# Mean square from token-major x, the phases' low part on ScalarE, the scan's last quarter behind three quarters of the GLU, and more warm matmuls

## Chip, cores and metric

One core of a Trainium2 chip runs the whole program. The metric is the device time of one launch in microseconds, the median of several runs.

## What is computed

A decoder block on 256 tokens of width 1024, in float32: an RMS norm, one wide input projection, causal attention of 8 heads beside a diagonal state-space scan (S5) with a gated linear unit, both merged by sigmoid gates, an output projection and a squared-ReLU MLP of width 4096, and a last RMS norm. Of the reference, cut:

```python
def rms_norm(x, g):
    y = xf * lax.rsqrt(jnp.mean(xf * xf, axis=-1, keepdims=True) + RMS_EPS)
    return (y * g.astype(jnp.float32)).astype(x.dtype)
...
h = rms_norm(x, g_mix)
z = h @ w_in            # q, k, v, u (scan input), two gates
a = moba_attention(rotary(q), rotary(k), v)     # one block of 256: plain causal
s = s5_branch(u, ...)   # scan, then gelu(y) @ w_glu, one half gates the other
x = x + (sigmoid(g_a) * a + sigmoid(g_b) * s) @ w_out
x = x + squared_relu(rms_norm(x, g_mlp) @ w_up) @ w_down
return rms_norm(x, g_final)
```

## The kernel before, in words

Each float32 product is made of three products in the type fp32r: a weight `w` is cast to `hi` on ScalarE (ACT, L83), VectorE (DVE) subtracts it to get `lo` (L84), the activations are split the same way, and TensorE (PE) adds hi·hi, hi·lo and lo·hi (`mm3` L87, `tok_mm` L264). A weight comes in units of 128x1024 float32 (512 KB) on SyncE's (SP's) DMA queue, in order (`w_load` L68), into five buffers; `hi` and `lo` have four buffers each.

The norm's scale is not applied to x. `xgh` and `xgl` are x times the gain, channel-major (`xT`), and the projections of them are multiplied by the tokens' factor `rs` behind the product. So PE can start before the mean square is known. The mean square is made from channel-major x: five ACT squares and three DVE additions into `sq` (L184 to L188), then PE multiplies the two remaining slices by a column of ones (`ms`, L202 to L206). DVE scales it into `rsm` (L208) and makes a first guess of the inverse root, GpSimd (POOL) does three Newton steps (`rsqrt`, L191); from it come `rs_half` (DVE, L213) and `rs_ps`, a broadcast by PE (L216).

The order of the program is: warm matmuls on zeros (L152), the scan's input projection `u` in eight slices of k (L160 to L182), then the steps of the string `ORDER` (L45): V is the projection `v` in units v00 to v03 (chunk 0) and v4 to v7 (chunk 1); P prepares the scan's coefficients (`prepare`, L358, some hundred 128x16 DVE operations named `s`, and the transposes `bt`, L470); T makes tables of cosines and sines (`tables`, L511); C is the second part of the coefficients; Q is a quarter of the scan (`ssm_quad`, L529); K are queries and keys with their rotation, S the scores, A the attention's output, G and B the gates; X loads a table of ACT functions, Y is the gelu of the scan's output. Then follow the GLU's quarters (L644), `w_out`, `w_up`, `w_down`.

A scheduler orders the instructions of each engine from this program order, from priorities (`tc.high_priority`, which the splits of weights have, with SPLIT_PRIO, and the Newton steps, with RSP) and from its own costs; each engine then runs its list in order. So an instruction that waits holds all that stand behind it on its engine.

The tables' phases are time times turn, in two parts. ACT writes the high part (L515), DVE takes the nearest whole turn from it (L516, L517), and adds the low part with four operations of 128x128 a table (L519).

Of the kernel before, what the change touches and what calls it, by code (L numbers as in the profile page):

```python
# [8 lines left out]
F32 = mybir.dt.float32  # L9
# [28 lines left out]
HEAT = 7  # L38
# [7 lines left out]
         "B0 G3 S3 X1 Y0 A3 B1")  # L46


def build(ctx, tc, dr, out):
# [93 lines left out]
    ones = keep.tile([P, 1], F32, name="ones")  # L143
    V.memset(ones, 1.0)
# [89 lines left out]
    V.tensor_mul(rcos, cos_c, rs)  # L234
    V.tensor_mul(rsin, sin_c, rs)
# [65 lines left out]
    scale = P ** -0.5  # L301
    mixA = p1.tile([P, KD, T], F32, name="mixA")

    def attn_head(q, k, j):
# [8 lines left out]
        V.tensor_reduce(st[:, 0:1], s[:, 0:128], axis=mybir.AxisListType.X, op=ALU.max)  # L313
        V.tensor_reduce(st[:, 1:2], s[:, 128:384], axis=mybir.AxisListType.X, op=ALU.max)
        V.tensor_scalar(st[:, 0:2], st[:, 0:2], -scale, None, op0=ALU.mult)
        pr = p1.tile([P, 384], F32, tag="pr", bufs=2, name="pr")
        act(pr[:, 0:128], s[:, 0:128], AF.Exp, bias=st[:, 0:1], scale=scale,
                     accum_out=st[:, 2:3])
        act(pr[:, 128:384], s[:, 128:384], AF.Exp, bias=st[:, 1:2], scale=scale,
# [281 lines left out]
    for step in ORDER.split():  # L601
# [24 lines left out]
        elif part == "Y":  # L626
            gelu()
# [16 lines left out]
    for q in range(4):  # L644
        acc = wide_banks(f"glu{q}") if q % 2 else [flat(mm_bank(f"glu{q}{h}")) for h in range(2)]
        for kk_ in range(2):
            wh, wl = w_unit(dr["w_glu"][2 * q + kk_], f"glu{q}{kk_}")
            for k2 in range(2):
                k, w = 2 * kk_ + k2, slice(k2 * 512, (k2 + 1) * 512)
                for hf in range(2):  # L650
                    tok_mm(acc[hf], wh[:, w], wl[:, w], yhl[0][:, 0:4], yhl[0][:, 4:8], k, hf,
                           k == 0, k == 3)
# [12 lines left out]
        split(mxh[:, two, :], mxl[:, two, :], mixA[:, two, :])  # L665
    ph1.__exit__(None, None, None)
# [213 lines left out]
```

## Time and profile before

| | |
|---|---|
| median of 3 runs | 404.85 us (404.71 to 405.25) |
| the profiled execution | 405.1 us, its span 403.2 us |
| PE busy | 394.3 us, 98% of the span |
| weight loads of PE | 355.2 us, beside the matmuls |
| DVE busy | 292.8 us, 73% |
| ACT busy | 225.9 us, 56% |
| POOL busy | 30.3 us, 8% |
| read from memory | 69.18 MB, 174 GB/s over the span |

The busy shares are averages over stages that differ. A row of the timeline gives the start of a group of like instructions, the time from the first one's start to the last one's end, their number, and in brackets how long the engine was idle before it and what released it. Matmuls overlap, so the distance from one start to the next is shorter than a row's duration; the same holds, by less, for DVE's and ACT's instructions.

### The profile page before, as it was taken

What the parts mean: (1) busy time and instruction counts of PE and PEld (TensorE: products, weight loads), DVE (VectorE), ACT (ScalarE), POOL (GpSimd) and SP (SyncE); (2) the same over time, 40 slices, a digit from 0 to 9 for tenths busy, and PEclk for the clock granted to TensorE, in tenths of its full rate; (3) what the DMA queues carried; (4) which work ended last, traced back from release to release, by engine and by line L of the source; (5) the groups of instructions that cost most, each with busy time, mean ns of one, the idle gap of its engine ahead of it and who ended that gap; (6) DMA issues with size and microseconds to landing.
All of it is one profiled execution on the core that took longest, in us unless ns stands there. A gap on an engine that the chain in (4) does not pass through costs nothing.

```text
span 403.2 us, 6862 instructions
## 1 busy us (share of the span) xinstructions
PE 394.3 (98%) x2635; PEld 355.2 (88%) x2635; DVE 292.8 (73%) x520; ACT 225.9 (56%) x360; POOL 30.3 (8%) x39
## 2 busy tenths in 40 slices
PE   8999999999999999999999999999999999999993
PEld 5988898989899787888889999999999888889983
DVE  5999999999999994769748665656565443564425
ACT  6767977655276557945647645464546334353323
POOL 4151492000000000000000000000000000000000
PEclk9999999999999999999999999999999999999998
DMA  8994843354516252456486465554555565555202
GB/s 228 401 337 149 246 154 102 111 202 151 192 56 208 84 195 102 158 159 206 161 308 209 152 215 191 176 194 172 191 178 193 172 205 169 199 192 178 101 0 104
DMA packets 23199, 71.57 MB, mean 178 GB/s; under 512 B 2944, under 2 KB 5248, under 8 KB 23168
## 3 DMA queue, kind: packets, MB, share of 16 engines
q1 hardware_dynamic: 20144, 68.92, 50.6%
q10 hardware_dynamic: 3024, 2.23, 1.9%
q8 instruction: 20, 0.33, 0.3%
q14 instruction: 11, 0.09, 0.1%
HBM read 69.18 MB, written 1.05 MB: 174 GB/s over the span
## 4 chain that ended last, share of the span: by engine, by line
PE 84%; DVE 5%; DMA 4%; ACT 2%; POOL 2%; issue 1%; ACTq 1%; SPq 0%; DVEq 0%
PE up L89 8%; PE up L90 8%; PE up L88 8%; PE dn L735 6%; PE dn L734 6%; PE dn L733 6%; PE k L88 2%; PE k L89 2%; PE k L90 2%; PE gb L268 2%; PE gb L266 2%; PE gb L267 2%; PE glu L268 2%; PE glu L266 2%; PE dnq L733 2%; PE dnq L735 2%
## 5 line engine op out<-in xcount | busy, mean ns | idle before, releaser
L89 PE MATMUL up<-x2l,hi_up 128*128 128x256 f32 x256 | 72.5, 284 | 0.0
L90 PE MATMUL up<-x2h,lo_up 128*128 128x256 f32 x256 | 72.3, 283 | 0.0
L88 PE MATMUL up<-x2h,hi_up 128*128 128x256 f32 x256 | 71.8, 283 | 0.0
L84 DVE TENSOR_TENSOR lo_dn<-raw_dn,hi_dn 128x1024 fp32r<-128x1024 f32 x32 | 39.2, 1225 | 44.0 <-ACT hi_dn L83 44.0
L83 ACT CAST hi_dn<-raw_dn 128x1024 fp32r<-128x1024 f32 x32 | 33.5, 1048 | 51.6 <-PE dn L735 25.8
L84 DVE TENSOR_TENSOR lo_up<-raw_up,hi_up 128x1024 fp32r<-128x1024 f32 x32 | 38.8, 1223 | 27.7 <-ACT hi_up L83 27.7
L83 ACT CAST hi_up<-raw_up 128x1024 fp32r<-128x1024 f32 x32 | 33.3, 1046 | 39.2 <-PE up L89 18.5
L89 PEld LDWEIGHTS up<-x2l,hi_up 128*128 128x128 f32 x256 | 49.1, 192 | 0.2 <-DVE x2l L694 0.2
L90 PEld LDWEIGHTS up<-x2h,lo_up 128*128 128x128 f32 x256 | 49.1, 192 | 0.0
L88 PEld LDWEIGHTS up<-x2h,hi_up 128*128 128x128 f32 x256 | 48.9, 192 | 0.1
L734 PE MATMUL dn<-lo_dn,hh 128*128 128x512 f32 x96 | 38.0, 395 | 0.0
L735 PE MATMUL dn<-hi_dn,hl 128*128 128x512 f32 x96 | 38.0, 395 | 0.0
L733 PE MATMUL dn<-hi_dn,hh 128*128 128x512 f32 x96 | 37.9, 395 | 0.0
L735 PEld LDWEIGHTS dn<-hi_dn,hl 128*128 128x128 f32 x96 | 18.0, 188 | 4.2
L733 PEld LDWEIGHTS dn<-hi_dn,hh 128*128 128x128 f32 x96 | 18.0, 188 | 3.8
L734 PEld LDWEIGHTS dn<-lo_dn,hh 128*128 128x128 f32 x96 | 18.0, 188 | 3.7
L89 PE MATMUL g<-xgl,hi_g 128*128 128x256 f32 x64 | 18.8, 294 | 0.0
L88 PE MATMUL k<-xgh,hi_k 128*128 128x256 f32 x64 | 18.4, 287 | 0.0
L90 PE MATMUL q<-xgh,lo_q 128*128 128x256 f32 x64 | 18.3, 286 | 0.0
L90 PE MATMUL g<-xgh,lo_g 128*128 128x256 f32 x64 | 18.3, 286 | 0.0
L90 PE MATMUL k<-xgh,lo_k 128*128 128x256 f32 x64 | 18.3, 286 | 0.0
L89 PE MATMUL q<-xgl,hi_q 128*128 128x256 f32 x64 | 18.3, 285 | 0.0
(267 smaller groups left out, 1046.9 us busy)
## 6 DMA issues: line engine op xcount, KB each, us to landing
raw_up<-w_up SPq DMA_DIRECT2D x32, 512.0 KB, 3.4
raw_dn<-w_down SPq DMA_DIRECT2D x32, 512.0 KB, 3.3
raw_v<-w_in SPq DMA_DIRECT2D x8, 512.0 KB, 6.0
raw_q<-w_in SPq DMA_DIRECT2D x8, 512.0 KB, 3.8
raw_k<-w_in SPq DMA_DIRECT2D x8, 512.0 KB, 3.2
raw_g<-w_in SPq DMA_DIRECT2D x8, 512.0 KB, 4.2
raw_gb<-w_in SPq DMA_DIRECT2D x8, 512.0 KB, 3.8
raw_glu<-w_glu SPq DMA_DIRECT2D x8, 512.0 KB, 3.2
```

The costliest lines, as they stand in the source:

```text
L83: ins = S.copy(hi, x).ins
L84: V.tensor_sub(lo, x, hi.bitcast(F32))
L88: PE.matmul(o, wh, xh, start=first, stop=False, **kw)
L89: PE.matmul(o, wh, xl, start=False, stop=False, **kw)
L90: PE.matmul(o, wl, xh, start=False, stop=last, **kw)
L266: PE.matmul(acc, xh[:, k, rows], wh, start=first, stop=False)
L267: PE.matmul(acc, xh[:, k, rows], wl, start=False, stop=False)
L268: PE.matmul(acc, xl[:, k, rows], wh, start=False, stop=last)
L733: PE.matmul(acc, xh, wh[:, w], start=(k == 0), stop=False, skip_group_check=True)
L734: PE.matmul(acc, xh, wl[:, w], start=False, stop=False, skip_group_check=True)
L735: PE.matmul(acc, xl, wh[:, w], start=False, stop=(k == 31), skip_group_check=True)
```

## The change

1. One more warm matmul of 512 columns (`HEAT` 8), and four more of 256, 256, 256 and 128 columns (`FILL`), each behind one of the first four matmuls of `u`.
2. The parameters `par` are transferred behind the second weight of `u`, not behind the first.
3. `sq`, its additions and the products `ms` are gone. Token-major x (`xtok`, 1 MB) is loaded behind unit v00 and ahead of the constants `cst`; ACT squares it in two operations that also give the sums `ss`, from which `rsm` comes.
4. The phases' low part is written by ACT (`ulo`, 16 operations of 128x128), and DVE adds it in one 128x512 operation a table, four in all, in place of sixteen.
5. The attention's scale goes into the rotation's tables, half of it on each side, and the row maxima are reduced with their sign turned. Eight small DVE operations go.
6. Gelu is made for three quarters of the scan's output; the first two GLU quarters multiply these (k 0 to 2), then come the last quarter's gelu, the last heads' output (A3), and then k 3.

```diff
-HEAT = 7
+HEAT = 8
+FILL = (256, 256, 256, 128)
...
-         "B0 G3 S3 X1 Y0 A3 B1")
+         "B0 G3 S3 X1 Y0 B1")
...
         if c == 0:
+            use_set(AF.Sin)
+        elif c == 1:
             nc.sync.dma_start(par, dr["par"])
-            use_set(AF.Sin)
     early = {0: w_load(dr["w_in"][0], "v00")}
+    xtok = p1.tile([P, 2, D], F32, tag="yhl", name="xtok")
+    nc.sync.dma_start(xtok, dr["x"].rearrange("(h p) d -> p h d", p=P))
...
+                    if k == 0 and i == 0:
+                        behind(mm, [hottest], "warm matmuls keep their place")
+                        hottest = warm(FILL[m])
+                        behind(hottest, [mm], "warm matmuls keep their place")
...
-    for i, xk in enumerate((x0, xT[:, 1, :])):
-        S.activation(sq[:, i, :], xk, AF.Square)
-    for c in range(1, 4):
-        S.activation(sq[:, 2 * c : 2 * c + 2, :], xT[:, 2 * c : 2 * c + 2, :], AF.Square)
-        V.tensor_add(sq[:, 0:2, :], sq[:, 0:2, :], sq[:, 2 * c : 2 * c + 2, :])
+    ss = p1.tile([P, 2], F32, name="ss")
+    for h in range(2):
+        S.activation(xtok[:, h, :], xtok[:, h, :], AF.Square, accum_out=ss[:, h : h + 1])
...
-    ms = att_bank("ms")
-    for h in range(2):
-        for i in range(2):
-            PE.matmul(ms[:, 0, h : h + 1], sq[:, i, h * P : (h + 1) * P], ones,
-                      start=(i == 0), stop=(i == 1))
-    V.tensor_scalar(rsm[:, 0:2], ms[:, 0, 0:2], 1.0 / D, EPS, op0=ALU.mult, op1=ALU.add)
+    V.tensor_scalar(rsm[:, 0:2], ss, 1.0 / D, EPS, op0=ALU.mult, op1=ALU.add)
...
-    V.tensor_mul(rcos, cos_c, rs)
+    V.scalar_tensor_tensor(rcos, cos_c, P ** -0.25, rs, op0=ALU.mult, op1=ALU.mult)
...
-        V.tensor_scalar(st[:, 0:2], st[:, 0:2], -scale, None, op0=ALU.mult)
...
+            S.activation(ulo[:, q, :], tpos, AF.Copy, scale=nlo[:, 4 * m + q : 4 * m + q + 1])
...
-        for q in range(4):
-            V.scalar_tensor_tensor(ang[:, q, :], tpos, nlo[:, 4 * m + q : 4 * m + q + 1],
-                                   ang[:, q, :], op0=ALU.mult, op1=ALU.add)
+        V.tensor_add(ang, ang, ulo)
...
+    first = [(q, glu_banks(q), glu_weights(q)) for q in range(2)]
+    for q, acc, ws in first:
+        glu_part(acc, ws, range(3))
+    gelu([3])
+    with tc.high_priority(ATT_PRIO):
+        attn_out(3, prs.pop(3), tha.pop(3))
+    for q, acc, ws in first:
+        glu_part(acc, ws, [3])
+        merge(q, acc)
```

How the lists of the engines move, at three places. In the names, numbers tell buffers apart; `s` is a 128x16 value of `prepare`, `q` the phases' high part, `tha` the phases.

ACT behind the last cast of `u`'s weights, before (hi_v_312 is v00's, and so on to v4's, v5's and v6's):

```order
L83 CAST hi_v_312<-raw_v_87 128x1024
L83 CAST hi_v_330<-raw_v_328 128x1024
L83 CAST hi_v_348<-raw_v_346 128x1024
L83 CAST hi_v_366<-raw_v_364 128x1024
L83 CAST hi_v_388<-raw_v_386 128x1024
L515 ACTIVATE q<-cst,s_536 128x128 x8
L83 CAST hi_v_406<-raw_v_404 128x1024
L515 ACTIVATE q<-cst,s_536 128x128 x4
L83 CAST hi_v_424<-raw_v_422 128x1024
```

and with the change (hi_v_306 is v00's, 324 v01's, 342 v02's, 360 v03's):

```order
L84 CAST hi_v_306<-raw_v_87 128x1024
L196 ACTIVATE xtok,ss<-xtok 128x1024 x2
L84 CAST hi_v_324<-raw_v_322 128x1024
L519 ACTIVATE q<-cst,s_530 128x128 x5
L520 ACTIVATE ulo<-cst,s_532 128x128 x4
L519 ACTIVATE q<-cst,s_530 128x128 x3
L84 CAST hi_v_342<-raw_v_340 128x1024
L84 CAST hi_v_360<-raw_v_358 128x1024
```

The squares stand between the first and the second cast of `v`, and twelve operations of the phases between the second and the third.

DVE from the low part of v00 on, before (lo_v_331 is v01's, 349 v02's, 367 v03's):

```order
L84 TENSOR_TENSOR lo_v_313<-raw_v_87,hi_v_312 128x1024
L388 SCALAR_TENSOR_TENSOR s_486<-s_484,s_472 128x16
L84 TENSOR_TENSOR lo_v_331<-raw_v_328,hi_v_330 128x1024
L388 SCALAR_TENSOR_TENSOR s_490<-s_486,s_488 128x16
L84 TENSOR_TENSOR lo_v_349<-raw_v_346,hi_v_348 128x1024
L383 TENSOR_TENSOR s_492<-par,s_490 128x16
L383 TENSOR_TENSOR s_522<-par,s_490 128x16
L378 TENSOR_SCALAR s_494<-s_492 128x16
L378 TENSOR_SCALAR s_524<-s_522 128x16
L84 TENSOR_TENSOR lo_v_367<-raw_v_364,hi_v_366 128x1024
L378 TENSOR_SCALAR s_496<-s_494 128x16
L208 TENSOR_SCALAR rsm<-ms 128x2
```

With the change, the end of the piece from `rsm` to the low part of v02 (lo_v_343):

```order
L216 TENSOR_SCALAR rs_half<-rsm 128x2
L379 TENSOR_SCALAR s_572<-s_514 128x16
L523 TENSOR_TENSOR tha<-tha,ulo 128x512
L391 SCALAR_TENSOR_TENSOR s_550<-s_548,s_534 128x16
L379 TENSOR_SCALAR s_564<-s_562 128x16
L521 TENSOR_SCALAR tha<-q 128x512
L386 TENSOR_TENSOR s_566<-s_514,s_550 128x16
L522 SCALAR_TENSOR_TENSOR tha<-tha,q 128x512
L386 TENSOR_TENSOR s_570<-s_566,s_550 128x16
L391 SCALAR_TENSOR_TENSOR s_576<-s_566,s_564 128x16
L85 TENSOR_TENSOR lo_v_343<-raw_v_340,hi_v_342 128x1024
```

Before, the low parts of v01, v02 and v03 stand ahead of `rsm`, with five small operations between them and one more behind. With the change `rsm` stands 21 rows ahead of v01's, and 21 rows, of which these are the last ten, stand between v01's and v02's.

SP's queue around x, before:

```order
L133 DMA raw_u_83<-w_u 128x512 x2
L70 DMA raw_v_87<-w_in 128x1024
L140 DMA cst<-cst 128x896
L70 DMA raw_v_328<-w_in 128x1024
L70 DMA raw_v_346<-w_in 128x1024
```

With the change:

```order
L71 DMA raw_v_87<-w_in 128x1024
L142 DMA xtok<-x 128x2x1024
L144 DMA cst<-cst 128x896
L71 DMA raw_v_322<-w_in 128x1024
L71 DMA raw_v_340<-w_in 128x1024
```

Each unit of `v` from the second on has 1 MB more ahead of it.

## Rows read from the trace of the kernel before

**Rows 1.** The page: busy us of each engine (share of the span) and instructions.
```profile
PE 394.3 (98%) x2635; PEld 355.2 (88%) x2635; DVE 292.8 (73%) x520; ACT 225.9 (56%) x360; POOL 30.3 (8%) x39
```

**Rows 2.** Timeline, PE: start, duration, engine, line, out<-in, count, [idle before <-releaser].
```profile
5.73 0.80 PE L180 MATMUL u_acc<-xgh,hi_u 128*128 128x256 f32 x2 [0.22 <-ACT hi_u L83]
...
8.89 1.05 PE L180 MATMUL u_acc<-xgl,hi_u 128*128 128x256 f32 x4
9.74 0.81 PE L180 MATMUL u_acc<-xgh,lo_u 128*128 128x256 f32 x4
10.39 0.64 PE L180 MATMUL u_acc<-xgh,hi_u 128*128 128x256 f32 x4
10.87 0.64 PE L180 MATMUL u_acc<-xgl,hi_u 128*128 128x256 f32 x4
```

**Rows 3.** Timeline from 15 to 20 us, ACT and PE.
```profile
15.24 1.05 ACT L83 CAST hi_v<-raw_v 128x1024 fp32r<-128x1024 f32 x1
...
17.64 1.05 ACT L83 CAST hi_v<-raw_v 128x1024 fp32r<-128x1024 f32 x1 [1.35 <-DMA raw_v<-w_in]
...
19.04 0.95 PE L205 MATMUL ms<-ones,sq 128*128 128x1 f32 x8
...
19.85 0.47 PE L266 MATMUL v<-hi_v,xgh 128*128 128x512 f32 x1
```

**Rows 4.** Timeline, PE around the transposes and the first scores.
```profile
47.63 0.28 PE L88 MATMUL q<-xgh,hi_q 128*128 128x256 f32 x1
48.48 1.09 PE L470 MATMUL bt<-cst,Bs 128*128 128x128 f32 x8 [0.58 <-POOL Bs L454]
...
65.72 0.46 PE L306 MATMUL s<-k,q 128*128 128x128 f32 x2 [0.34 <-DVE k L298]
```

**Rows 5.** Windows: stretch, its us, busy us (count) by engine, PEclk, DMA share, GB/s.
```profile
30.00:45.00 15.00, 15.00 (x79) 12.84 (x79) 15.00 (x40) 11.64 (x19) 1.97 (x2) 1.00 0.57 185
```

**Rows 6.** Timeline at 216 us: squares with sums on ACT, and DVE's reader.
```profile
216.67 1.06 ACT L697 ACTIVATE sq<-x2t 128x1024 f32<-128x1024 f32 x1
...
219.03 0.17 DVE L698 TENSOR_SCALAR st<-st 128x2 f32<-128x2 f32 x1 [0.36 <-ACT sq L697]
```

**Rows 7.** Timeline from 22 to 30 us, DVE.
```profile
22.75 0.15 DVE L208 TENSOR_SCALAR rsm<-ms 128x2 f32<-128x2 f32 x1
...
24.56 0.97 DVE L388 SCALAR_TENSOR_TENSOR s<-s,s 128x16 f32<-128x16 f32 x10
25.45 1.21 DVE L84 TENSOR_TENSOR lo_v<-raw_v,hi_v 128x1024 fp32r<-128x1024 f32 x1
...
27.94 0.17 DVE L213 TENSOR_SCALAR rs_half<-rsm 128x2 f32<-128x2 f32 x1 [0.67 <-POOL rsm L200]
...
28.35 0.68 DVE L517 SCALAR_TENSOR_TENSOR tha<-tha,q 128x512 f32<-128x512 f32 x1
...
29.57 0.41 DVE L516 TENSOR_SCALAR tha<-q 128x512 f32<-128x512 f32 x1
```

**Rows 8.** Timeline, POOL: two of the Newton steps on `rsm`.
```profile
25.69 1.03 POOL L200 TENSOR_TENSOR rsm<-rsm 128x2 f32<-128x2 f32 x1
...
27.71 0.20 POOL L200 TENSOR_TENSOR rsm<-rsm 128x2 f32<-128x2 f32 x1
```

**Rows 9.** Timeline, ACT: the phases' high part.
```profile
24.27 2.46 ACT L515 ACTIVATE q<-cst,s 128x128 f32<-128x128 f32 x8 [0.32 <-DVE s L415]
```

**Rows 10.** Timeline, PE: unit v03 and the broadcast of the scale.
```profile
28.14 0.39 PE L266 MATMUL v<-hi_v,xgh 128*128 128x512 f32 x1
...
29.50 0.60 PE L216 MATMUL rs_ps<-cst,rsm 128*128 128x128 f32 x4
...
30.17 0.39 PE L267 MATMUL v<-lo_v,xgh 128*128 128x512 f32 x1
```

**Rows 11.** Windows behind the last matmul.
```profile
397.00:398.00 1.00, 0.05 (x1) 0.00 (x0) 0.88 (x2) 0.39 (x2) 0.00 (x0) 1.00 0.91 342
...
399.00:399.30 0.30, 0.00 (x0) 0.00 (x0) 0.27 (x2) 0.18 (x1) 0.00 (x0) 0.92 0.00 0
```

More of the change, by code (lines that the diff above doesn't have):

```diff
@@ L151, in build, with warm @@
     hot = att_bank("hot").rearrange("p a b -> p (a b)")
+    def warm(n):
+        return PE.matmul(hot[:, 0:n], heat[:, 0:P], heat[:, 0:n], start=True, stop=True).ins
     for i in range(HEAT):
-        PE.matmul(hot, heat[:, 0:P], heat, start=True, stop=True)
+        hottest = warm(512)
     xgh = keep.tile([P, KD, T], F32R, tag="xh", name="xgh")
     xgl = keep.tile([P, KD, T], F32R, tag="xl", name="xgl")
-    sq = p1.tile([P, KD, T], F32, tag="yhl", name="sq")
     u_acc = ps.tile([P, 2, 2, T], F32, tag="x", name="u_acc")
@@ L179, in build @@
                 for m in range(4):
-                    PE.matmul(u_acc[:, m // 2, m % 2, :], w[:, ws[m]], x[:, k, :],
-                              start=(k == 0 and i == 0 and m % 2 == 0),
-                              stop=(k == KD - 1 and i == 2), skip_group_check=True)
-    for i, xk in enumerate((x0, xT[:, 1, :])):
-        S.activation(sq[:, i, :], xk, AF.Square)
-    for c in range(1, 4):
-        S.activation(sq[:, 2 * c : 2 * c + 2, :], xT[:, 2 * c : 2 * c + 2, :], AF.Square)
-        V.tensor_add(sq[:, 0:2, :], sq[:, 0:2, :], sq[:, 2 * c : 2 * c + 2, :])
+                    mm = PE.matmul(u_acc[:, m // 2, m % 2, :], w[:, ws[m]], x[:, k, :],
+                                   start=(k == 0 and i == 0 and m % 2 == 0),
+                                   stop=(k == KD - 1 and i == 2), skip_group_check=True).ins
+                    if k == 0 and i == 0:
[5 more added lines that the diff above has]
+        S.activation(xtok[:, h, :], xtok[:, h, :], AF.Square, accum_out=ss[:, h : h + 1])
     def rsqrt(eng, dst, m, tmp):
@@ L233, in build @@
         V.tensor_mul(u[:, 2 * c : 2 * c + 2], by_parity(u_acc[:, c]), rs_par)
-    V.tensor_mul(rcos, cos_c, rs)
-    V.tensor_mul(rsin, sin_c, rs)
+    V.scalar_tensor_tensor(rcos, cos_c, P ** -0.25, rs, op0=ALU.mult, op1=ALU.mult)
+    V.scalar_tensor_tensor(rsin, sin_c, P ** -0.25, rs, op0=ALU.mult, op1=ALU.mult)
     for q in range(4):
@@ L299, in rope @@
         return o
-    scale = P ** -0.5
     mixA = p1.tile([P, KD, T], F32, name="mixA")
@@ L312, in attn_head @@
         st = p1.tile([P, 6], F32, tag="st", bufs=2, name="st")
[L313 to L315 removed]
+        V.tensor_reduce(st[:, 0:1], s[:, 0:128], axis=mybir.AxisListType.X, op=ALU.max,
+                        negate=True)
+        V.tensor_reduce(st[:, 1:2], s[:, 128:384], axis=mybir.AxisListType.X, op=ALU.max,
+                        negate=True)
         pr = p1.tile([P, 384], F32, tag="pr", bufs=2, name="pr")
[L317 removed]
+        act(pr[:, 0:128], s[:, 0:128], AF.Exp, bias=st[:, 0:1],
                      accum_out=st[:, 2:3])
[L319 removed]
+        act(pr[:, 128:384], s[:, 128:384], AF.Exp, bias=st[:, 1:2],
                      accum_out=st[:, 3:4])
@@ L512, in tables @@
         hi, nlo = ssm[-2:]
+        ulo = rot("ulo")
         uhi, ang, cs, sn = rot("q", QK), rot("tha", 2), rot("cs", 4), rot("sn", 4)
@@ L589, in build, with gelu @@
     yhl = []
-    def gelu():
-        yhl.append(p1.tile([P, KD, T], F32R, tag="yhl", name="yhl"))
+    def gelu(ms):
+        if not yhl:
+            yhl.append(p1.tile([P, KD, T], F32R, tag="yhl", name="yhl"))
         yflat = yT.rearrange("p m e j -> p m (e j)")
-        for m in range(4):
+        for m in ms:
             act(yflat[:, m, :], yflat[:, m, :], AF.Gelu_apprx_tanh)
@@ L626, in build @@
         elif part == "Y":
-            gelu()
+            gelu(range(3))
         elif part == "Q":
@@ L642, in wide_banks, with glu_weights, glu_banks, glu_part @@
         return [flat(b[:, h]) for h in range(2)]
[L644 to L652, printed above, removed]
+    def glu_weights(q):
+        return [w_unit(dr["w_glu"][2 * q + kk_], f"glu{q}{kk_}") for kk_ in range(2)]
+    def glu_banks(q):
+        return wide_banks(f"glu{q}") if q % 2 else [flat(mm_bank(f"glu{q}{h}")) for h in range(2)]
+    def glu_part(acc, ws, ks):
+        for k in ks:
+            w = slice(k % 2 * 512, (k % 2 + 1) * 512)
+            for hf in range(2):
+                tok_mm(acc[hf], ws[k // 2][0][:, w], ws[k // 2][1][:, w],
+                       yhl[0][:, 0:4], yhl[0][:, 4:8], k, hf, k == 0, k == 3)
+    def merge(q, acc):
         tp = att_bank(f"mt{q}")
@@ L665, in build @@
         split(mxh[:, two, :], mxl[:, two, :], mixA[:, two, :])
+    first = [(q, glu_banks(q), glu_weights(q)) for q in range(2)]
[7 more added lines that the diff above has]
+        merge(q, acc)
+    for q in (2, 3):
+        acc = glu_banks(q)
+        glu_part(acc, glu_weights(q), range(4))
+        merge(q, acc)
     ph1.__exit__(None, None, None)
```

2 lines of the change are left out of this document (removed).

## The prediction

> **What bounds the kernel now.** The page's busy table comes first: TensorE (PE) is busy 394.3 us of a 403.2 us span [rows 1], so a saving on another engine is worth only the PE wait that it ends, and a burden on another engine costs only once it is later than PE. I therefore went through PE's timeline for its waits. There are three places. In the head the first projection `u` waits until 5.73 for ScalarE's (ACT's) second cast of the weight, and four of its 256-column matmuls take 0.85 us (8.89 to 9.74), but only 0.48 us after 10.39 (to 10.87): PE works at half clock there, and is raised at about 10.1 [rows 2]. Then PE runs without a pause through the mean square's matmuls `ms` (19.04) into projection `v` (19.85), whose weights arrive on one queue: ACT starts the cast of unit v00 at 15.24 and of v01, for which it waits on the transfer, at 17.64 [rows 3]. The other two places are the transposes `bt`, which wait for GpSimd (POOL), and the scores `s`, which wait for VectorE (DVE): the last matmul before `bt` starts at 47.63 and steps 0.12, so 0.73 us are lost before 48.48, 0.15 more than the idle 0.58 of the row, which counts from a pipelined end; before `s` the row shows 0.34, so 0.50 are lost [rows 4]. The rest of the span has no wait of this size, down to the last matmul. Around the first of them DVE has no pause (15.00 us busy of 15.00 from 30 to 45, PE too) [rows 5]: PE lives there on the lead of the weights' casts and subtractions.
>
> **The change part by part.** *Warm matmuls and parameters.* The eighth 128x512 one and the fills' 896 columns are 5.5 times 256 columns, at half clock (0.85 for four) at most 1.2 us, of which the wait of 0.22 before 5.73 hides a part; if they raise the clock as soon as PE stops pausing at 5.73 and not at 10.1, half of these 4.4 us comes back [rows 2]. The removed `ms` kept PE from 19.04 to 19.85. So `v` could start between 17 and 20.0 (19.04 + 1.2 − 0.22). What follows shows that any start up to 20.0 gives the same end, so I cost the head at nothing. The parameters' transfer moves behind one weight; its first DVE reader is some 16-column operations between longer ones, nothing waits for them before 20 us.
>
> *Token-major x.* It is 1.05 MB on the queue between v00 and the constants. Between the starts at 15.24 and 17.64, 0.98 MB of constants and v01 landed, 0.41 MB per us, so x takes 2.56 us: it is there at 17.80, the constants at 18.9 in place of 16.3, v01 at 20.20 in place of 17.64 [rows 3]. The two squares with their sums are an operation that the kernel already has later: from the first one's start (216.67) to the DVE instruction that reads the sums (219.03) 2.36 us pass [rows 6]. So DVE's `rsm` can run at 20.16. It ran at 22.75 before [rows 7], but now it stands ahead of lo_v1, the low part of v01.
>
> *DVE's list.* Its steps are 0.07 to 0.08 us shorter than the durations: ten small 16-column operations of 0.16 take 0.97, so 0.09 each; a weight's low part (1.21) steps 1.13, the 128x512 `scalar_tensor_tensor` (0.68) 0.60, the 128x512 `tensor_scalar` (0.41) 0.33 [rows 7]. From `rsm` to lo_v1 there are 21 small rows (1.89): lo_v1 runs 22.05 to 23.18. Its cast, 1.0 us from 20.20, is in time. Between lo_v1 and lo_v2, where there was one small row, 21 rows now stand: 16 small (1.44), two `tensor_scalar` (0.66), two `scalar_tensor_tensor` (1.20) and one of the new 128x512 adds. The trace has no such add from SBUF alone; its bounds are the 0.33 and the 0.60 of these rows, and I take 0.60, since two streams are read. That is 3.90, so lo_v2 would be done at 23.18 + 3.90 + 1.13 = 28.21. One of these rows, `rs_half`, waits for POOL's Newton steps, which took 5.19 us from `rsm` (22.75) to `rs_half` (27.94). DVE comes to it at 24.92 (nine small rows, 0.33, 0.60 behind 23.18), POOL at 20.16 + 5.19 = 25.35: 0.43 more, **lo_v2 is done at 28.64**. Of these 5.19 one POOL step took 1.03 where others of its kind took 0.20, while DVE subtracted a weight's low part (from 25.45 on) [rows 7, 8]. Without that, 4.4 us, DVE waits for nothing: 28.2; with two such steps the end is 29.3. I take the one, because lo_v1 falls into the new chain.
>
> Here a rule of the Trainium skill speaks against the change ("SBUF — State Buffer", section "Who interferes with whom"): a DVE instruction with two SBUF inputs contends with a GpSimd one that reads SBUF, because the second input comes through a shared read interface. The row of 1.03 us agrees. By the rule the two 0.60 us operations behind lo_v1 hold POOL too, and the time would lie near the upper of the two ends.
>
> *ACT's list.* Behind hi_v1 (21.2) stand eight `q` and four of the sixteen new `ulo` operations, ahead of hi_v2. Eight of the kind took 2.46 us, 0.30 a step [rows 9]; twelve are 3.6: hi_v2 runs 24.8 to 25.85. It is late, but not last: lo_v2 is.
>
> *PE.* `v` steps 0.227 us (six matmuls from 28.14 to 29.50) [rows 10]. Unit v00 has twelve, 2.72; from 20.0 it ends at 22.7, two matmuls of v01 fit before lo_v1 at 23.18, as claimed above. Ten remain: 25.45; the broadcast `rs_ps` (0.44, from 29.50 and 30.17), 25.9; two of v02 to 26.35; then a **wait of 2.3 us for lo_v2**; ten more to 30.91. There v03 starts. Before, it started at 28.14 with `rs_ps` still ahead, so the lag is 30.91 − 28.14 − 0.44 = **2.33 us**. lo_v3 and lo_v4 follow lo_v2 directly and stay in front of PE.
>
> *What is given back.* A PE that comes 2.3 us later finds Bs ready (0.74 back) and the keys rotated (0.50 back) [rows 4]; the smaller DVE work (sixteen 128x128 operations become four adds) helps both. The four later `ulo` groups fill ACT's pauses before 62 us; I cost them at nothing, since these pauses are waits for DVE or PE, and if a cast is late there instead, 0.5 us more. The scale folded into the rotation tables and the negated maxima shorten the way to the exponentials, where PE does not wait.
>
> *The scan's last quarter.* PE has no wait there now, and the three quarters of the products that come first keep it occupied. Nothing gained, nothing lost.
>
> **Sum:** 405.1 + 2.33 − 0.74 − 0.50 = 406.2 against the profiled execution, which is 0.25 us over the median; against the median **406.0 us**. With the ends for lo_v2, 28.2 and 29.3: 405.5 to 406.6; with the wait of `s` not given back 407.1, with a late cast 407.6.
>
> **The rivals.** *The clock falls in the wait.* At the end of the kernel PE stops at 397.05, and the granted clock is down from 1.0 to 0.5 (2.4 to 1.2 GHz) at about 399.25, 2.2 us later [rows 11]. The new wait is 2.3 us and follows shorter ones. If it falls, `v` runs at half speed until the clock is raised; in the head that took 4.4 us from the last pause (5.73 to 10.1), in which PE does 0.48/0.85 of the work [rows 2]: 1.9 us more, 407.9. [...]
>
> *No change.* The lag is a long chain of small steps. If the squares' result and POOL are each half a microsecond earlier than rated and the adds take 0.33, lo_v2 is done at about 27.5 and the time is 404.9. The rate of the queue and the step of the small rows speak against it.
>
> *Faster.* If lo_v2 is done before 26.75, the lag is below 0.44 and the returned waits of 1.24 us outweigh it: at 26.0 the time is 403.3, and with no wait but that for v01's transfer (20.20) not below 402.1. This needs the squares not to hold the DVE list: x landing beside v00 instead of behind it, so that `rsm` runs near 18. For it: the transfers of a queue are spread over sixteen engines. Against: landings in the trace come in order at the queue's full rate [rows 3]. The change not doing what it says is part of this and the last case: the warm matmuls may leave the clock where it is, which costs nothing.
>
> **How the numbers follow.** The forecast has 0.45, the fallen clock 0.20, no change 0.20, faster 0.15. A difference within 0.2% (0.81 us, 404.04 to 405.66) is about what a measurement here can't tell from none; 0.05 of the forecast's own spread (405.5 upwards) lies in it. So faster 0.15, same 0.25, slower 0.60. The forecast's own range is 405.5 to 407.6; the range reaches up to the fallen clock with a little of the late cast, 408.3, and down to 404.3, which takes in the no-change case and leaves out the faster one.
>
> **What would show it.** Right: `rsm` at about 20.2, POOL's steps ending near 25.3, hi_v2 at 24.8, a PE wait for lo_v2 of over 2 us before 28.7, no wait before `bt`. Wrong: lo_v2 before 27, or PE waiting elsewhere for more than 1 us. The clock's rival shows as a granted clock below 1.0 between 28 and 35 us and a step twice 0.227 in `v`; if `rsm` runs before 19, the queue was misread.

## The result and the profile after

The changed kernel takes 407.83 us (median of 6 runs, 406.97 to 408.48); the ratio to the kernel before is **1.0072, 95% interval 1.0057 to 1.0087**: slower by 2.9 us. The profiled execution is the shortest of the six, 406.97 us with a span of 405.2, against 405.1 and 403.2 before. (Ratios here are formed by rounds and can differ in the third digit from a quotient of medians.)

The page of the changed kernel, busy time by engine:

```profile
PE 393.1 (97%) x2632; PEld 352.8 (87%) x2632; DVE 287.8 (71%) x496; ACT 231.1 (57%) x375; POOL 34.8 (9%) x39
```

PE is busy 1.2 us less than before [rows 1] and yet the span is 2.0 us longer. So PE waits more. The view of PE's waits, summed over the span (engine, line, what it waited for, total, times, longest):

```profile
PE v L270 <- DVE lo_v L85: 2.2, 2, 1.6
...
PE v L269 <- ACT hi_v L84: 1.1, 2, 0.9
PE u_acc L185 <- ACT hi_u L84: 0.8, 1, 0.8
PE bt L473 <- POOL Bs L457: 0.5, 1, 0.5
```

Two waits are new, both in `v`: for the low parts and for the casts. That for `s` [rows 4] is gone, that for `bt` isn't. The timeline of PE has them in order (columns as in [rows 2]):

```profile
9.00 0.74 PE L185 MATMUL u_acc<-xgh,hi_u 128*128 128x256 f32 x4 [0.80 <-ACT hi_u L84]
...
17.82 0.40 PE L269 MATMUL v<-hi_v,xgh 128*128 128x512 f32 x1
...
21.66 0.73 PE L269 MATMUL v<-hi_v,xgh 128*128 128x512 f32 x2 [0.94 <-ACT hi_v L84]
22.96 0.50 PE L270 MATMUL v<-lo_v,xgh 128*128 128x512 f32 x1 [0.56 <-DVE lo_v L85]
...
26.13 0.73 PE L269 MATMUL v<-hi_v,xgh 128*128 128x512 f32 x2 [0.16 <-ACT hi_v L84]
28.46 0.50 PE L270 MATMUL v<-lo_v,xgh 128*128 128x512 f32 x1 [1.60 <-DVE lo_v L85]
...
30.90 1.07 PE L269 MATMUL v<-hi_v,xgh 128*128 128x512 f32 x4
...
44.53 0.39 PE L271 MATMUL v<-hi_v,xgl 128*128 128x512 f32 x1
45.42 1.09 PE L473 MATMUL bt<-cst,Bs 128*128 128x128 f32 x8 [0.50 <-POOL Bs L457]
...
75.51 0.38 PE L308 MATMUL s<-k,q 128*128 128x128 f32 x2
```

`v` starts at 17.82, 2.03 us earlier than before [rows 3]. Unit v03 starts at 30.90, 2.76 later than before [rows 10], 2.32 if the 0.44 of `rs_ps`, which stood behind it before, are taken off. The head's gain is lost in four waits, counted from one start to the next less the step: 1.09 (v01's cast), 0.73 (its low part), 0.32 (v02's cast) and 1.76 us (its low part), 3.90 together; the other 0.45 is the first step behind each wait, 0.34 long in place of 0.23. DVE shows why the last is the longest:

```profile
19.09 0.17 DVE L211 TENSOR_SCALAR rsm<-ss 128x2 f32<-128x2 f32 x1
...
21.64 1.26 DVE L85 TENSOR_TENSOR lo_v<-raw_v,hi_v 128x1024 fp32r<-128x1024 f32 x1 [0.55 <-ACT hi_v L84]
...
25.03 0.17 DVE L216 TENSOR_SCALAR rs_half<-rsm 128x2 f32<-128x2 f32 x1 [0.41 <-POOL rsm L208]
...
25.19 0.69 DVE L523 TENSOR_TENSOR tha<-tha,ulo 128x512 f32<-128x512 f32 x1
...
27.19 1.22 DVE L85 TENSOR_TENSOR lo_v<-raw_v,hi_v 128x1024 fp32r<-128x1024 f32 x1
...
38.33 0.41 DVE L449 TENSOR_TENSOR ab<-ab,cw 128x256 f32<-128x256 f32 x1
...
73.51 0.68 DVE L301 TENSOR_TENSOR k<-k,sw 128x512 f32<-128x512 f32 x1
```

Between the low parts of v01 (21.64) and v02 (27.19) lie the 21 rows that the list puts there, the wait for POOL's Newton steps among them. (The last two rows belong to the waits for `bt` and `s`, below.) On ACT the squares of x come first, then the late cast of v01, and later still those of v02 and v03:

```profile
16.87 1.06 ACT L196 ACTIVATE xtok<-xtok 128x1024 f32<-128x1024 f32 x1 [1.42 <-DMA xtok<-x]
...
20.57 1.04 ACT L84 CAST hi_v<-raw_v 128x1024 fp32r<-128x1024 f32 x1 [1.51 <-DVE s L379]
...
25.04 1.98 ACT L84 CAST hi_v<-raw_v 128x1024 fp32r<-128x1024 f32 x2
```

POOL first has a step of the Newton chain that takes 1.06 us where most others take 0.2, as before [rows 8], then the two operations that fill Bs with `bpad`, and the four that write `ab` into it:

```profile
21.91 1.06 POOL L207 TENSOR_SCALAR rsm<-rsm 128x2 f32<-128x2 f32 x1
...
24.80 0.19 POOL L208 TENSOR_TENSOR rsm<-rsm 128x2 f32<-128x2 f32 x1
...
33.19 10.45 POOL L465 TENSOR_SCALAR Bs<-bpad 128x512 f32<-128x512 f32 x2 [8.19 <-DMA bpad<-bpad]
43.60 4.61 POOL L457 TENSOR_SCALAR Bs<-ab 64x256 f32<-64x256 f32 x4
```

The pair's data came at 33.19, and it took 10.45 us; before, it started at 28.47 and took 3.50. PE loses 0.66 us before `bt` (44.53 to 45.42, less a step of 0.23), nearly the 0.73 of before, but it isn't the same wait. Before, POOL had long been done with the pair and sat idle until DVE had added up `ab` (the row names the small operation behind that addition):

```profile
44.66 0.41 DVE L446 TENSOR_TENSOR ab<-ab,cw 128x256 f32<-128x256 f32 x1
...
45.16 5.60 POOL L454 TENSOR_SCALAR Bs<-ab 64x256 f32<-64x256 f32 x4 [13.19 <-DVE s L383]
```

With the change `ab` is ready at 38.74, and POOL is held by its own pair until 43.6. PE's list has changed there too. Before, 46 matmuls of `q` stand ahead of `bt`; with the change there are two, and `bt` follows v07 directly. So PE comes to `bt` 3.0 us earlier than before (44.76, not 47.75), and Bs is ready 3.06 us earlier (45.42, not 48.48). The scores `s` stand later, at 75.51 and not 65.72, behind 96 matmuls of the gate `g` where 42 stood: the keys are complete 8.6 us later than before (74.2, not 65.6), and PE still needn't wait for them. The last matmul ends at 398.90, 1.85 us after the 397.05 of before [rows 11]. The sum of the parts is close to that: 2.32 behind at v03, less the 0.50 of `s` and the 0.07 of `bt`, is 1.75.

### The profile page after: what moved, and what is told of

It reads as the page before. It is cut to its first block, busy times and chain, and to the rows that moved or that the text cites. A ratio compares the mean times of both kernels' runs of the same rounds, so it can differ in the third digit from the quotient of the medians.

```text
span 405.2 us, 6839 instructions
## 1 busy us (share of the span) xinstructions
PE 393.1 (97%) x2632; PEld 352.8 (87%) x2632; DVE 287.8 (71%) x496; ACT 231.1 (57%) x375; POOL 34.8 (9%) x39
## 4 chain that ended last, share of the span: by engine, by line
PE 87%; POOL 4%; DMA 4%; DVE 2%; issue 1%; ACT 1%; SPq 1%; ACTq 0%
PE up L90 8%; PE up L91 8%; PE up L89 8%; PE dn L758 6%; PE dn L759 6%; PE dn L757 6%; POOL Bs L465 3%; PE k L91 2%; PE g L91 2%; PE g L89 2%; PE q L91 2%; PE k L89 2%; PE k L90 2%; PE g L90 2%; PE gb L269 2%; PE q L89 2%
## 5 line engine op out<-in xcount | busy, mean ns | idle before, releaser
L89 PE MATMUL g<-xgh,hi_g 128*128 128x256 f32 x64 | 18.4, 288 | 0.0
L89 PE MATMUL q<-xgh,hi_q 128*128 128x256 f32 x64 | 18.2, 285 | 0.0
```

The lines of the kernel that those rows point to most:

```text
L89: PE.matmul(o, wh, xh, start=first, stop=False, **kw)
```

## The experiments

**First with the edits alone.** Each of the first four kernels was written as an edit of the source, and the scheduler made its lists anew.

*e1_old_ms:* the changed kernel with the mean square as it was before, and no x.

```diff
-    nc.sync.dma_start(xtok, dr["x"].rearrange("(h p) d -> p h d", p=P))
...
+        S.activation(sq[:, 2 * c : 2 * c + 2, :], xT[:, 2 * c : 2 * c + 2, :], AF.Square)
...
+            PE.matmul(ms[:, 0, h : h + 1], sq[:, i, h * P : (h + 1) * P], ones,
```

> The changed kernel with its mean square made as before (squares of channel-major x, products `ms`), and no token-major x on the queue; all other parts of the change stay. Theory (the loss comes from x on the queue and from `rsm` ahead of v01's low part): in the scheduler's new list the low parts of v01 to v6 stand ahead of the tables' operations, so no wait of PE in `v` over 0.5 us, POOL's Bs starts before 30 us again, and the time falls by 3 to 4 us to 404 to 405. Rival (the phases' low part on ACT is the burden): 406 or more, with PE waiting for a cast. Second rival (the warm matmuls' clock): no change, 407 to 408.

Measured: 419.59 us, ratio 1.0371 (1.0355 to 1.0386): missed. The timeline of PE has a wait of 4.5 us before `bt`, one of 2.6 in `up` and several smaller ones, far from the edit:

```profile
48.75 1.54 PE L481 MATMUL bt<-cst,Bs 128*128 128x128 f32 x6 [4.54 <-POOL Bs L465]
```

*e4_head_alone:* the kernel before with parts 1 and 2.

```diff
+HEAT = 8
+FILL = (256, 256, 256, 128)
...
+        elif c == 1:
             nc.sync.dma_start(par, dr["par"])
```

> The kernel before with only the warm matmuls (8 and the four fills) and the later transfer of the parameters. Theory (the head raises the clock some 4 us earlier, so `v` starts 0.5 to 1.1 us earlier, and PE then waits that much longer for Bs before the transposes `bt`): within 0.4 us of the kernel before. Rival (the start of `v` is what counts): 403.8 to 404.4. Second rival (the fills delay `u`): 405.3 or more.

Measured: 413.52 us, ratio 1.0218 (1.0203 to 1.0234): missed. Most of the loss is one wait in the attention, again nowhere near the edit:

```profile
173.10 0.47 PE L338 MATMUL pt<-cst,pr 128*128 128x128 f32 x1 [6.91 <-ACT pr L331]
```

*e5_fill_wait:* the changed kernel with eight warm matmuls of 512 columns in the wait for v02's low part.

```diff
+STUFF = 8
...
+                            for _ in range(STUFF):
+                                mm = warm(512)
```

> The changed kernel with eight more warm matmuls of 512 columns in the wait for v02's low part, behind the two matmuls that come before it; they add nothing to the output. They take 1.9 us of a wait of 1.8 to 2.0. Rival of the prediction (in some executions the clock falls in that wait, which makes the runs of 408.3 beside those of 407.0): the runs lie together at 406.9 to 407.3. Theory without the clock (the wait alone): the same spread from 407.0 to 408.5, and the median 407.6 to 408.0.

Measured: 409.53 us (408.19 to 411.1), ratio 1.012 (1.0096 to 1.0144): missed. `rsm` ran 1.9 us later than in the changed kernel (20.99), the chain on POOL ended 2.5 us later (`rs_half` at 27.56), and PE waits for that chain as well, so the run says nothing of the clock.

*e3_old_low:* the changed kernel with the phases' low part on DVE again.

```diff
-            S.activation(ulo[:, q, :], tpos, AF.Copy, scale=nlo[:, 4 * m + q : 4 * m + q + 1])
...
-        V.tensor_add(ang, ang, ulo)
+        for q in range(4):
+            V.scalar_tensor_tensor(ang[:, q, :], tpos, nlo[:, 4 * m + q : 4 * m + q + 1],
+                                   ang[:, q, :], op0=ALU.mult, op1=ALU.add)
```

> The changed kernel with the phases' low part on DVE again, in four 128x128 operations a table; ACT has none of the `ulo`. Theory (x on the queue, and the tables' operations ahead of v02's low part): the order behind `rsm` stays, only one add of 0.60 becomes four steps of 0.26, and three of the small rows go: lo_v2 is done within 0.6 us of the changed kernel's, time 407.0 to 408.0. Rival (the low part on ACT is the burden): hi_v2 is cast 1.2 us earlier and the time falls to 405.5 or less.

Measured: 407.59 us (405.46 to 409.51), ratio 1.0067 (1.0043 to 1.0091), as the theory had it: the order behind `rsm` stays, and so does PE's wait for v02's low part, 1.94 us. (Its new list has `bt` behind `q` again, at 51.62, and there is no wait before it.) Its trace shows something that the trace of the changed kernel doesn't. The window behind that wait (columns as in [rows 5], PEclk is the third from the end):

```profile
28.00:31.00 3.00, 2.40 (x6) 1.92 (x7) 3.00 (x5) 2.93 (x5) 0.00 (x0) 0.62 0.51 154
```

The granted clock has a mean of 0.62 there: it was at the lower of its two levels (1.2 and 2.4 GHz) for most of the stretch. And POOL's pair for Bs starts at the same 33.19, but takes less than half as long:

```profile
33.19 4.69 POOL L465 TENSOR_SCALAR Bs<-bpad 128x512 f32<-128x512 f32 x2 [7.59 <-DMA bpad<-bpad]
```

What follows from the four: an edit of a line isn't one change here. It moves instructions all over the lists, and the large waits of e1 and e4, far from the edits, are read as that. In all that follows the lists were therefore **pinned**: each engine's instructions are chained, by dependencies that only fix the order, in the order of the kernel started from, and nothing but the named instructions is moved, added or taken out.

*e8_warm_alone:* the kernel before, with part 1 alone.

```diff
-HEAT = 7
+HEAT = 8
+FILL = (256, 256, 256, 128)
```

> The kernel before with its lists fixed as they were, and the eighth and the four filling warm matmuls added to PE's. Theory (PE reaches full pace at about 6 us and not at 10, and `v` starts 0.5 to 1 us earlier, but the wait for Bs takes it over): 404.4 to 405.1, the wait before the transposes 0.5 us or more longer. Rival (it is worth what `v` gains): 403.8 to 404.3.

Measured: 405.53 us, ratio 1.0002 (0.9986 to 1.0017): no difference that can be told. In the profile PE has full pace earlier and loses the time again, in two waits of 0.5 us for `u`'s weights and one in front of v07's low part:

```profile
41.27 0.50 PE L275 MATMUL v<-lo_v,xgh 128*128 128x512 f32 x1 [1.05 <-DVE lo_v L85]
```

The wait before `bt` is no longer than before (0.77 us), so the theory had the place wrong. The profile is of one of the two longest of the twelve executions (406.44 us), and in it v03's cast came 1.53 us later than before and v07's low part 1.24, so its waits aren't those of the median. The ratio stands by itself: a head that is faster on PE alone gains nothing here.

*e9_x_alone:* the kernel before, with part 3 alone. Its `rsm` stays behind the low part of v03.

```diff
+    nc.sync.dma_start(xtok, dr["x"].rearrange("(h p) d -> p h d", p=P))
...
+        S.activation(xtok[:, h, :], xtok[:, h, :], AF.Square, accum_out=ss[:, h : h + 1])
...
-            PE.matmul(ms[:, 0, h : h + 1], sq[:, i, h * P : (h + 1) * P], ones,
```

> The kernel before with its lists fixed as they were, and the mean square from token-major x: x behind v00 on the queue, two squares on ACT behind v00's cast, no `sq` and no `ms`. `rsm` keeps its place behind v03's low part. Theory (x ahead of v01 delays `v` by 1 to 1.5 us, and `rs_ps`, which waits for a later mean square, by as much; the missing `ms` gives 0.8 back): 405.5 to 406.8. Rival (only the new list costs, x on the queue does not): within 0.4 us of the kernel before.

Measured: 408.08 us (407.75 to 408.34), ratio 1.0059 (1.0039 to 1.0078): slower, as expected, by more than the 405.5 to 406.8 of the theory and by about as much as the whole change. Its ACT waits for each weight behind x:

```profile
20.59 1.05 ACT L83 CAST hi_v<-raw_v 128x1024 fp32r<-128x1024 f32 x1 [0.26 <-DMA raw_v<-w_in]
21.86 1.05 ACT L83 CAST hi_v<-raw_v 128x1024 fp32r<-128x1024 f32 x1 [0.22 <-DMA raw_v<-w_in]
23.14 1.05 ACT L83 CAST hi_v<-raw_v 128x1024 fp32r<-128x1024 f32 x1 [0.23 <-DMA raw_v<-w_in]
```

v01 to v03 come every 1.27 us; v01's cast starts 2.95 us later than before [rows 3]. Of this, 0.41 was there at v00 already (15.65), and 2.54 is x: from v00's cast to v01's 4.94 us pass, not 2.40. DVE follows:

```profile
24.48 1.23 DVE L84 TENSOR_TENSOR lo_v<-raw_v,hi_v 128x1024 fp32r<-128x1024 f32 x1
25.70 0.16 DVE L200 TENSOR_SCALAR rsm<-ss 128x2 f32<-128x2 f32 x1
...
30.85 0.56 DVE L205 TENSOR_SCALAR rs_half<-rsm 128x2 f32<-128x2 f32 x1 [0.66 <-POOL rsm L197]
...
38.38 1.28 DVE L225 TENSOR_TENSOR u<-u_acc,xg 128x512 f32<-128x512 f32 x2
...
41.69 1.22 DVE L84 TENSOR_TENSOR lo_v<-raw_v,hi_v 128x1024 fp32r<-128x1024 f32 x1
```

`rsm` comes 2.95 us later than before and `rs_half` 2.91 later [rows 7]; the multiplication of `u`, at 35.45 before, is 2.93 later, and so is the low part of v07, which was at 38.76. PE, itself late by then, still waits 1.31 us for it, as much as for `rs_ps` (1.21) and more than for v01's low part (0.60), where before it waited for none:

```profile
22.95 0.50 PE L259 MATMUL v<-lo_v,xgh 128*128 128x512 f32 x1 [0.45 <-DVE lo_v L84]
...
30.87 0.38 PE L208 MATMUL rs_ps<-cst,rsm 128*128 128x128 f32 x1 [1.05 <-POOL rsm L197]
...
42.96 0.50 PE L259 MATMUL v<-lo_v,xgh 128*128 128x512 f32 x1 [1.15 <-DVE lo_v L84]
```

So the mean square from token-major x, tried alone, costs about what the whole change costs: in this order of DVE's list through the late low part of v03 and the late `rsm` behind it, in the changed kernel's through the late low parts. That it is x's place ahead of v01 is read from the casts, which wait for their weights.

*e6_lows_first:* the changed kernel, with the casts and low parts of v02 and v03 ahead of the tables' work.

```diff
 L84 CAST hi_v_324<-raw_v_322 128x1024
+L84 CAST hi_v_342<-raw_v_340 128x1024
+L84 CAST hi_v_360<-raw_v_358 128x1024
 L519 ACTIVATE q<-cst,s_530 128x128 x5
...
-L521 TENSOR_SCALAR tha<-q 128x512
+L85 TENSOR_TENSOR lo_v_343<-raw_v_340,hi_v_342 128x1024
...
+L85 TENSOR_TENSOR lo_v_361<-raw_v_358,hi_v_360 128x1024
+L521 TENSOR_SCALAR tha<-q 128x512
+L522 SCALAR_TENSOR_TENSOR tha<-tha,q 128x512
+L216 TENSOR_SCALAR rs_half<-rsm 128x2
```

> The changed kernel with every engine's list fixed as its scheduler made it, but for these moves: on ACT the casts of v02 and v03 stand directly behind that of v01 and v04's ahead of the next table's operations; on DVE the low parts of v02 and v03 stand ahead of the tables' operations; on PE two matmuls of v04 stand behind v03. The computation and the transfers are the same. Theory (the lists: tables ahead of weights): the wait for v02's low part (1.8 us) is gone, the queue is freed some 4 us earlier so that bpad lands before 30 us, and the time is 404.6 to 405.8; if the wait for Bs before the transposes takes all of it over, 406.5 to 407. Rival (x on the queue ahead of v01 is the cost): 406.8 or more, only the waits for v01 matter.

Measured: 408.74 us (406.62 to 410.49), ratio 1.0073 (1.0044 to 1.0102): the theory missed, and the time lies where the rival, x on the queue, had it. The profile is of a short execution (406.78 us); what makes the median 2 us longer isn't shown. The wait for v02's low part is gone, and 1.50 us are lost on POOL's chain instead; those for v01 stay:

```profile
27.51 0.71 PE L219 MATMUL rs_ps<-cst,rsm 128*128 128x128 f32 x4 [1.34 <-POOL rsm L208]
```

With v02's low part earlier, Bs's data come earlier too, the pair takes 4.82 us, and `bt`, in the same place of PE's list, doesn't wait:

```profile
30.74 4.82 POOL L465 TENSOR_SCALAR Bs<-bpad 128x512 f32<-128x512 f32 x2 [3.29 <-DMA bpad<-bpad]
```

*e7_x_behind_v03:* e6 with x behind v03 on the queue, `rsm` behind v03's low part, `rs_ps` behind v04 and `bt` behind `q`.

```diff
-L142 DMA xtok<-x 128x2x1024
...
 L71 DMA raw_v_358<-w_in 128x1024
+L142 DMA xtok<-x 128x2x1024
```

> As the last one, and token-major x is transferred behind v03 and not ahead of v01; the squares stand on ACT behind v03's cast, `rsm` on DVE behind v03's low part, `rs_ps` on PE behind v04, and the first transposes behind the second unit of queries, as in the kernel before. Theory (both x's place on the queue and the list): no wait of PE in `v`, which runs from 17.8 to 40 us, and 402 to 404. Rival (DVE and ACT are full up to 62 us, a wait comes back later): a wait of over 1 us between 40 and 62 us, and 404.5 to 405.5.

Measured: 411.33 us, ratio 1.0136 (1.0112 to 1.016): missed. No wait is left in v00 to v03, but the scale comes later. `rs_ps` costs PE 1.29 us behind v04, and `u`'s multiplications, which need the scale, come at 38.91, with the low part of v07 behind them. That of `q` stands behind an addition of the tables, for which DVE waits for ACT:

```profile
42.25 0.50 PE L270 MATMUL v<-lo_v,xgh 128*128 128x512 f32 x1 [2.23 <-DVE lo_v L85]
...
50.90 0.58 PE L91 MATMUL q<-xgh,lo_q 128*128 128x256 f32 x1 [3.23 <-DVE lo_q L85]
```

and on DVE:

```profile
49.02 0.69 DVE L523 TENSOR_TENSOR tha<-tha,ulo 128x512 f32<-128x512 f32 x1 [5.49 <-ACT ulo L520]
```

ACT's cast of `q`, ahead of that `ulo`, came only at 45.63; how much of this second wait the late scale causes wasn't tried. As far as the two orders show, x early delays the weights and x late delays the scale; the mean square from channel-major x needs neither.

*e11_low_alone:* the kernel before, with part 4 alone, its ACT operations put where they delay no weight.

```diff
+            S.activation(ulo[:, q, :], tpos, AF.Copy, scale=nlo[:, 4 * m + q : 4 * m + q + 1])
...
+        V.tensor_add(ang, ang, ulo)
```

> The kernel before with its lists fixed as they were and the phases' low part on ACT: four `ulo` operations a table on ACT, behind the first eight `q`, behind the two absolute values of tables 0 and 1, and behind the last four `q`; on DVE one 128x512 addition where the last of four 128x128 operations stood. Theory (the part is harmless where it delays no weight, and frees 1.3 us of DVE before Bs): 404.0 to 404.9. Rival (ACT becomes late): 405.5 or more, with a wait of PE for a cast before 62 us.

Measured: 404.42 us, ratio 0.999 (0.9979 to 1.0001): no difference that can be told. PE's waits before `bt` (0.68 us) and `s` (0.42) remain.

*e10_two_moves:* the kernel before, with two DVE instructions moved, each of which the wait before `bt` or `s` ends on.

```diff
 L444 TENSOR_TENSOR ab_612<-bc,s_584 128x256
+L446 TENSOR_TENSOR ab_612<-ab_612,cw 128x256
...
 L519 SCALAR_TENSOR_TENSOR tha<-cst,s_538,tha 128x128 x4
-L446 TENSOR_TENSOR ab_612<-ab_612,cw 128x256
...
+L298 TENSOR_TENSOR k<-k,sw 128x512
 L519 SCALAR_TENSOR_TENSOR tha<-cst,s_538,tha 128x128 x4
-L298 TENSOR_TENSOR k<-k,sw 128x512
```

> The kernel before with its lists fixed as they were, but for two moves on DVE: the addition that completes the first part for Bs stands directly behind its product, ahead of the second query unit's low part and of four phase operations; and the addition that completes the rotated keys stands ahead of four phase operations. Nothing of the change is in it. Theory (only PE's waits are worth time; these two are 0.73 and 0.50 us): the wait before `bt` goes, that before `s` shrinks to 0.2 us, 403.6 to 404.2. Rival (they are hidden or come back elsewhere): within 0.3 us of the kernel before.

Measured: 404.37 us, ratio 0.9988 (0.9976 to 1.0001): between the theory and the rival, and no difference that can be told. Both waits are gone from PE's timeline; 0.86 us come back at 77.82, where `pt` waits for ACT.

*e12_both:* e11 and e10 together.

> The last two together: the two moves, and the low part on ACT. Theory: 403.4 to 404.2, no wait of PE over 0.3 us between 20 and 70 us. Rival: no better than the better one of the two.

Measured: 403.44 us, ratio **0.9965 (0.995 to 0.998)**: faster than both kernels. Neither row has a wait any more, and none comes at `pt`:

```profile
47.30 1.04 PE L470 MATMUL bt<-cst,Bs 128*128 128x128 f32 x8
...
64.39 0.38 PE L306 MATMUL s<-k,q 128*128 128x128 f32 x2
```

*after_again:* the changed kernel once more, with no edit.

> The changed kernel once more, for its spread. If the clock falls in the wait for v02's low part in some executions, the runs lie in two groups about 1.3 us apart, and a profile of one of the later group shows `v` at steps of 0.43 us behind the wait; otherwise the differences lie in when the transfers land.

Measured: 407.91 us (407.03 to 409.21), ratio 1.0079 (1.0057 to 1.01). This time the profiled execution took 407.94 us. The executions don't fall into two clean groups (the longest is 409.21). The same stretch behind the wait for v02's low part, first in the execution of 406.97 us, then in this one:

```profile
28.00:31.00 3.00, 2.54 (x11) 2.09 (x12) 3.00 (x9) 3.00 (x7) 0.00 (x0) 1.00 0.50 175
```

```profile
28.00:31.00 3.00, 2.22 (x5) 1.82 (x6) 3.00 (x9) 3.00 (x8) 0.00 (x0) 0.58 0.38 115
```

and PE's timeline in this one:

```profile
28.78 0.80 PE L270 MATMUL v<-lo_v,xgh 128*128 128x512 f32 x1 [2.12 <-DVE lo_v L85]
...
31.08 0.63 PE L270 MATMUL v<-lo_v,xgh 128*128 128x512 f32 x1
...
31.91 0.39 PE L269 MATMUL v<-hi_v,xgh 128*128 128x512 f32 x1
...
32.60 1.09 PE L269 MATMUL v<-hi_v,xgh 128*128 128x512 f32 x4
```

PE lost 2.28 us in the wait, then stepped 0.43 a matmul up to 31.5, and 0.23 after that. Ten matmuls took 3.82 us (28.78 to 32.60), where they took 2.44 in the first profile (28.46 to 30.90): the fallen clock cost 1.38 us. v03 starts 1.70 us later than in the first profile and the last matmul ends 0.96 later, at 399.86, because `bt` waits no longer.

## Why the prediction was right, and where it was off

The direction was right, and so were the place and the price of the delay in `v`: slower, by the wait for v02's low part. The time fell into the range (404.3 to 408.3), but 1.8 us above the forecast of 406.0: the loss is 2.9 us where 1.15 were forecast, because of a wait that was wrongly booked as returned and of a fallen clock that was held for an alternative. Of the signs named, no wait before `bt` failed, and the PE wait of over 2 us for v02's low part held in the second profile (2.28) and not in the first (1.76).

**The head.** Any start of `v` between 17 and 20.0 was to give the same end; it started at 17.82, and the gain was lost by v02. In e8 part 1 alone gains nothing either. Right. One reading needs a caution: the half clock before 10.1 us was read from the matmuls' steps of 0.21 us. The granted clock on record is 1.00 over all of 0 to 12 us in the profile of the kernel before, so the record doesn't show it.

**x and `rsm`.** x was put at 17.80 and `rsm` at 20.16; the first square started at 16.87 and `rsm` ran at 19.09. Both are about a microsecond early, and the queue was 0.84 ahead already at v00, whose cast began at 14.40, not at 15.24 [rows 3]. From v00's cast x took 2.47 us, as rated (2.56). But v01, rated to be there at 20.20, was cast from 20.57 on, and its low part waited 0.55 us for that. The cost of x on the queue is borne out by e9.

**DVE's list.** The low part of v02 was to be done at 28.64: it started at 27.19, and the next row at 28.32. `rs_half` was put at 25.35 with a wait of 0.43; it ran at 25.03 with 0.41. That is two errors that cancel: `rsm` ran 1.07 us early, and POOL's chain from it took 5.94 us, not 5.19. The upper end of 29.3 didn't come: beside the `scalar_tensor_tensor` at 23.67 one POOL step took 0.52 us, beside v01's low part one took 1.06. The new add steps 0.60 (25.19, next row 25.79), the bound that was taken. The second cast, put at 24.8, ran at 25.04.

**PE.** v03 was put at 30.91 and the lag at 2.33 us: 30.90 and 2.32. That it came out so closely has some luck in it: the single waits were otherwise spread (1.09, 0.73, 0.32, 1.76 for the one of 2.3), because the head was faster and v01 waited more.

**What is given back: the term that failed.** "A PE that comes 2.3 us later finds Bs ready (0.74 back) and the keys rotated (0.50 back)" took both instructions to be where they had stood in PE's list, and what they wait for to come at its old time. The scheduler had moved both. PE came to `bt` 3.0 us earlier than before, not 2.3 later, and 0.74 didn't come back, although Bs was ready 3.06 us earlier.

What Bs waited for had changed as well. Before, it was DVE's `ab`, as e10 confirms, which ends the wait by moving that addition. With the change it was POOL's pair: bpad stands on SP's queue behind weights that wait for buffers which the low parts free (it was issued at 28.81, right behind v07's transfer, which waited for v02's low part until 28.4), it came 4.7 us later, and the pair took 10.45 us. With a pair of 3.50 Bs would have been ready before 41 us (an estimate: `ab` at 38.74, and the 1.82 from 43.60 to 45.42), and in its old place, 44 matmuls of `q` later, `bt` would have come behind it too; e6 and e3 show one of each without a wait.

The 0.50 of `s` came back, but not for the stated reason: `s` stands 9.8 us later in time, and the keys come 8.6 us later. That is luck. With 0.74 not returned the sum for the profiled execution is 406.9, and it took 406.97.

On that pair the trace sides with the Trainium skill ("SBUF — State Buffer", section "Who interferes with whom") in direction: DVE was busy 9.3 of the 11 us from 33 to 44, mostly with two-input operations, and the page says that these contend with a GpSimd instruction that reads SBUF. The size is not explained: in e3 the same pair, from the same 33.19 on, with DVE busy all along, beside low parts and other two-input operations too, took 4.69. It isn't chance of one execution, since the changed kernel's second profile has 10.54 and e5 10.36. What makes the difference stays open.

**The clock: a rival that happens in some executions.** The rival was priced at 1.9 us over the forecast, 407.9, and given 0.20. It isn't an alternative to the forecast but comes on top of it from one execution to the next. Of the two profiles of the changed kernel one has it and one hasn't; of its twelve timed executions eight lie at 407.85 or above and three at 406.97 to 407.04. That the eight are those with the fall is read from the two profiles and shown for none of the others. The mean granted clock of each execution supports it for five of the eight (0.991 to 0.995, where the four shortest have 0.997 or 0.998); the other three have 0.996 or 0.997, and what makes them longer is open. The fall costs 1.38 us in `v`, less than the 1.9, and PE's delay behind it returns the wait at `bt`. The first profile without the fall took 406.97, the second with it 407.94. That the median, 407.83, lies at the rival's 407.9 is partly luck: the rival's sum has a dearer fall (1.9) on a forecast that books 0.74 too much as returned.

On the two, the Trainium skill ("TensorE: Matmul & The Clock Gate", section "Part 1: The HAM clock gate (the "warmup" mystery)") says of a kernel's start that the number of slow matmuls differs from run to run. Here the same is seen in `v`, in the middle of work: behind the same wait, none in one execution and about seven in another.

**The other parts.** Part 4, costed at nothing, makes no difference alone (e11), and taking it out of the changed kernel makes none either (e3). Part 6, costed at nothing: neither trace has a PE wait from 70 us to the last matmul that the view of waits lists. Parts 2, 5 and 6 were not tried alone.

**The faster case**, with x landing beside v00, is ruled out by the squares, which wait for x until 2.47 us behind v00's cast, and by e9's casts, which wait for the weights behind x one after the other.

## What to carry to other kernels

A transfer that feeds a small early result still costs its full bytes to everything behind it on the queue: here 1 MB for 256 sums moved every later weight of the projection, and in the orders tried the order of the readers only chose which engine showed the wait. Before a wait is booked as returned, look up where the waiting instruction stands in the new list, and follow the awaited data back to what it waits for there: here both had moved. In a kernel whose lists a scheduler makes, pin the lists before trying one part; otherwise the experiment measures the scheduler.

## What the runs showed that was not expected

- A pair of 128x512 POOL operations of the same shapes took 2.98 to 4.82 us in eleven of the fourteen profiles and 10.36 to 10.54 in three, those of the changed kernel (twice) and of e5. What in the work beside it makes the difference wasn't found.
- The clock fell after a PE wait of 1.94 us (e3) and of 2.28 (after_again), with shorter waits ahead of it, and didn't in the profile where PE lost 1.76 at the same place. In e6 PE lost 1.50 there and the clock stayed at 1.00; in e7 it lost 2.39 before v07's low part and the clock stayed at 1.00 (42 to 45 us), then 3.38 before `q`, and the clock was at 0.50 (51 to 54 us). So the length of the last wait alone doesn't tell whether it falls.
- Edits of a few lines moved the time by +8.7 (e4) and +14.7 us (e1) through the scheduler's lists, more than any part of the change was worth.
- Moving two DVE instructions past table work (e10) ended two PE waits, but a third came up at `pt`; with part 4 beside it (e12) that one was gone too, and 1.4 us came out. The intervals don't tell whether this is more than the sum of the two; why `pt` no longer waits was not followed up.
